# Two pieces of side work moved in a tuned decoder block: the squares of x and the batched heads' key selection

## The chip, the cores and the metric

The kernel runs on one core of one Trainium2 chip. The metric is device time of one execution, in microseconds (us). The time before is the median of three runs, and one further run was taken with the hardware profiler; every row quoted below comes from that profiled run. TensorE is PE in the profile (PEld its weight loads), VectorE is DVE, ScalarE is ACT, GpSimd is POOL, SyncE is SP.

## The reference

One decoder block over 1024 tokens of width 1024, float32. Gated linear attention (GLA) and a spatial gating branch run beside each other and are merged; behind them stands PEER, a mixer that picks 16 of 16384 one-neuron experts for each of eight heads by product keys. Cut to what matters here:

```python
h = modulate(rms_norm(x, norm1_w), shift1, scale1)      # needs mean(x*x) of every row
q, k, v, r, a_lr, su, sv, g_a, g_b = split(h @ w_in)
o = gla_chunked(q, k, v, log_sigmoid(a_lr @ w_alpha_up + b_alpha) / 16)
merged = sigmoid(g_a) * rms_norm(o) * silu(r) + sigmoid(g_b) * spatial_gating(gelu(su), gelu(sv))
x = x + gate1 * (merged @ w_out)
h2 = modulate(rms_norm(x, norm2_w), shift2, scale2)
# PEER: scores of two key halves, top 16 of each, top 16 of the sums, softmax, experts
s1, s2 = q1 @ keys1.T, q2 @ keys2.T                     # q1, q2 = halves of h2 @ w_q, 8 heads
v1, i1 = top_k(s1, 16); v2, i2 = top_k(s2, 16)
top_s, pos = top_k(v1[:, None] + v2[None, :], 16)
y = sum(softmax(top_s) * gelu(u_idx . h2) * v_idx)
out = rms_norm(x + gate2 * y, final_norm_w)
```

## The kernel before, in words

The tokens are worked in two halves of 512 (`hf` 0 and 1), each as four blocks of 128. Every projection is a **group**: 512 output columns, eight steps k over the 1024 inputs, four PSUM tiles. A step loads a 128x512 weight tile `wt` (SP queue, line 1250), splits it into `wh` (ACT, line 1253) and `wl` (DVE, line 1254), and runs twelve matmuls. The split runs three steps ahead (`LOOK`), with four buffers each for the loads and for the split tiles. Behind the eighth step come the four evictions, and the next group's matmuls need the PSUM tiles that these free.

One half runs, in this order: value groups V0 and V1; query/key groups QK0 and QK1, each followed by two GLA heads; the gating groups; the output projection; and then the four **query groups** of PEER, `w_q(0)` to `w_q(3)`. A query group's evictions copy PSUM to `qt` on ACT (line 1607); `s_part` multiplies `qt` by the keys (line 1655, PSUM pool `aux`, two buffers), copies the scores to `so` (line 1657) and selects the best eight of each key half on DVE (lines 200, 201).

`x_prep` gets the second half's first norm ready inside the first half. It loads four blocks of x as rows (`xb`, line 1175), squares each on ACT with a row sum (line 1176), turns the sums into one reciprocal root per token (`rstd_row`: DVE and POOL, a matmul into `aux` at line 1165, a copy to `rrow` at line 1167), loads x transposed (`xt`, line 1182) and multiplies it by `rrow` on DVE (line 1184, eight products). At the start of the second half `h_split` turns these into `hTh` (ACT, line 1211) and `hTl` (DVE, lines 1215 and 1216), which the value group V0 reads. Before the change the whole of `x_prep` is called behind `w_q(1)`.

The selection of experts has two ways. Most heads take at most eight of each key half (`route`); a (token, head) pair whose eighth weight still counts is gathered into a batch of 128 such pairs per half, and `rare` does a full top-16 for them: it builds the list, fetches their scores from DRAM into `qsc` by an indirect DMA on POOL (line 428), runs `tops16` on both key halves (lines 204 to 208), then `select16`, `gates` and `pack_rare`, whose result goes to DRAM (lines 293 and 294) and is read back at line 507 when `peer_stream` opens.

The order on each engine comes from three things. Generators (`route`, `pack_half`, `rare` in the queue `qr`; `direct_rows` in `qdir`; `peer_stream` in `qp`) are advanced by `step()`, behind each step k of a group, and `qr` runs its first generator only; so the program order of side work is fixed by counts of steps. The tile framework's scheduler then takes the program order as priority and places each instruction on its engine by its own timeline. And `tc.issue_after(ins)` puts the block's instructions behind `ins` in the order of that instruction's engine; it orders issue, it is no wait of its own. What comes out is one fixed order for each engine, in which each instruction waits for its inputs.

`direct_rows`, which computes each token's first expert of every head, uses the same pool of eight row buffers (`b4`) as `xb` and fetches two 512 KB tiles for each head (line 752).

Of the kernel before, what the change touches and what calls it, by code (L numbers as in the profile page):

```python
# [17 lines left out]
P = 128  # L18
# [62 lines left out]
def block_kernel(ctx: ExitStack, tc: tile.TileContext, x, xT, cT, w_ada, b_ada, b_adaT, n1T, w_inp, w_alr,  # L81
# [256 lines left out]
    def route(hf, q, tsel, tv, ti):  # L338
# [48 lines left out]
        nc.vector.tensor_copy(tsel[:, :, c0:c0 + 2 * K1], w[:, :, 0].rearrange("p (b k) -> p b k", b=BH))  # L387
        yield

    def rare(gi, rps):  # L390
        nb = len(GROUPS[gi])
        n, col = nb * PH, NBLK + NG + gi
        f = flags[gi].rearrange("p b h -> p (b h)")
        inc = r2.tile([P, n], F32, name="qinc")
        tq = r2.tile([P, n + 4], F32R, name="tq")
        nc.vector.tensor_tensor_scan(inc, ones[:, :n], f, 0.0, op0=OP.mult, op1=OP.add)
        nc.vector.tensor_tensor(tq[:, 0:n], inc, f, op=OP.mult)
        nc.vector.tensor_copy(cnt[:, col:col + 1], inc[:, n - 1:n])
        pst = rps.tile([P, 1], F32, name="aux", tag="aux")
        nc.tensor.matmul(pst, ltri, cnt[:, col:col + 1], start=True, stop=True)  # L400
        se = r2.tile([P, 2], F32, name="qse")
        nc.vector.tensor_copy(se[:, 0:1], pst)
        nc.vector.tensor_tensor(se[:, 1:2], se[:, 0:1], cnt[:, col:col + 1], op=OP.add)
        nc.scalar.activation(tq[:, n:n + 1], se[:, 0:1], AF.Identity, scale=-1.0)
        nc.scalar.activation(tq[:, n + 1:n + 2], lane1, AF.Identity, bias=-1.0)
        nc.scalar.activation(tq[:, n + 2:n + 4], ones[:, 0:2], AF.Identity)
        lt = r2.tile([P, P], F32, name="qlt", tag="cidx")
        E = r2.tile([P, P], F32R, name="qE", tag="th")
        nc.vector.tensor_scalar(lt, iota[:, :P], se[:, 1:2], None, op0=OP.is_lt)
        nc.vector.scalar_tensor_tensor(E, iota[:, :P], se[:, 0:1], lt, op0=OP.is_ge, op1=OP.mult)  # L410
        yield
        tps = rps.tile([P, n + 4], F32, name="tpq", tag="aux")
        nc.tensor.matmul(tps, E, tq, start=True, stop=True)
        tt = r2.tile([P, n + 4], F32, name="qt")
        nc.scalar.activation(tt, tps, AF.Identity)
        r = r2.tile([P, 4], F32, name="qr")
        nc.vector.tensor_tensor(r[:, 0:1], tt[:, n:n + 1], lane1, op=OP.add)
        nc.vector.scalar_tensor_tensor(inc, tt[:, 0:n], r[:, 0:1], ctab[:, :nb].rearrange("p b h -> p (b h)"),
                                       op0=OP.is_equal, op1=OP.mult, accum_out=r[:, 1:2])
        nc.vector.scalar_tensor_tensor(r[:, 2:3], tt[:, n + 1:n + 2], float(PH), r[:, 1:2], op0=OP.mult, op1=OP.add)  # L420
        ix = r2.tile([P, 1], I32, name="qix")
        nc.vector.tensor_copy(ix, r[:, 2:3])
        nc.vector.tensor_scalar(rtok[gi], ix, 3, None, op0=OP.logical_shift_right)
        nc.vector.tensor_copy(r[:, 3:4], rtok[gi])
        for i in range(nb):
            nc.vector.tensor_scalar(rcol[gi][:, i:i + 1], r[:, 3:4], -float(i * P), None, op0=OP.add)
        sc = rp.tile([P, 2, NK], F32, name="qsc", tag="bits")
        nc.gpsimd.indirect_dma_start(out=sc.rearrange("p c k -> p (c k)"), out_offset=None,
                                     in_=s_g[gi].rearrange("b p (h k) -> (b p h) k", h=PH),
                                     in_offset=bass.IndirectOffsetOnAxis(ap=ix, axis=0))  # L430
        yield
        tv = r2.tile([P, 1, 2, TOPK], F32, name="qtv")
        ti = r2.tile([P, 1, 2, TOPK], U32, name="qti")
        for c in range(2):
            tops16(tv[:, 0, c], ti[:, 0, c], sc[:, c])
        yield
        ts, sel = yield from select16(r2, tv, ti, 1, "q")
        tsel = r2.tile([P, 3 * TOPK + 2], F32, name="qtsel")
        dd, sm = yield from gates(r2, ts, 1, TOPK, "q")
        nc.vector.tensor_tensor(sm, sm, tt[:, n + 2:n + 3], op=OP.mult)  # L440
        nc.vector.tensor_scalar(tsel[:, 2 * TOPK:3 * TOPK], dd[:, 0], sm, None, op0=OP.mult)
        nc.vector.scalar_tensor_tensor(tsel[:, TOPK:2 * TOPK], sel[:, 0], float(NK), sel[:, 1], op0=OP.mult, op1=OP.add)
        yield
        yield from pack_rare(tsel, TOPK, NBLK + gi, rps, "q")
        yield
# [607 lines left out]
    with ExitStack() as pa:  # L1053
# [113 lines left out]
            nc.scalar.activation(rrow, rps, AF.Identity)  # L1167
            return rrow

        def x_prep(t0):  # L1170
            ss = sm_p.tile([P, BH], F32, name="ss")
            for i in range(BH):
                xb = t4("xb")
                with tc.issue_after(last_wt[0]):
                    nc.sync.dma_start(xb, x[t0 + i * P:t0 + (i + 1) * P, :])
                nc.scalar.activation(xb, xb, AF.Square, accum_out=ss[:, i:i + 1])
            rrow = rstd_row(ss, nc.vector)
            xts = []
            for k in range(0, KD, 2):
                xt = v4.tile([P, 2, HALF], F32, name="xt", tag="v4")  # L1180
                with tc.issue_after(last_wt[0]):
                    nc.sync.dma_start(xt, xT[k * P:(k + 2) * P, t0:t0 + HALF].rearrange("(a p) t -> p a t", p=P))
                for kk in range(2):
                    nc.vector.tensor_tensor(xt[:, kk], xt[:, kk], rrow, op=OP.mult)
                    xts.append(xt[:, kk])
            return xts
# [50 lines left out]
            at.append(a)  # L1237

        order_ = (G_V0, G_V1, G_QK0, G_QK1, G_SV0, G_SV1, G_R0, G_R1, G_A0, G_A1, G_SU0, G_SU1, G_B0, G_B1)
        plan, made, last_wt = [], [], []  # L1240
        for _ in range(NHALF):
            plan += [(w_inp[g], k) for g in order_ for k in range(KD)]
            plan += [(w_outp[m], k) for _ in range(2) for k in range(KD) for m in range(2)]
# [13 lines left out]
        for hf in range(NHALF):  # L1257
# [108 lines left out]
            def ev_qk(hp):  # L1366
                def f(i, ps):
                    h = 2 * hp + i % 2
                    G, eg, p4 = G16[h], eglt[h], v4c(ps)

                    def last(c):
                        return eg[:, :, c:c + 1].to_broadcast([P, 4, 64])

                    if i < 2:
                        eG = t2("eG")
                        with tc.issue_after(last_vt[0]):
                            nc.scalar.activation(eG, G, AF.Exp, scale=1.0 / TAU)
                        e4 = v4c(eG)
                        qs = gl.tile([P, HALF], F32, name="qs")
                        q1 = gl.tile([P, 4, 64], F32, name="q1")  # L1380
                        q4 = v4c(qs)
                        nc.vector.scalar_tensor_tensor(q4[:, :, 0], p4[:, :, 0], DK ** -0.5, e4[:, :, 0], op0=OP.mult, op1=OP.mult)
                        nc.vector.scalar_tensor_tensor(q1, p4[:, :, 1], DK ** -0.5, e4[:, :, 1], op0=OP.mult, op1=OP.mult)  # L1383
                        nc.vector.tensor_tensor(q4[:, :, 1], q1, last(0), op=OP.mult)
                        qk[h] = [qs, q1]
                    else:
                        kk = gl.tile([P, 4, 3, 64], F32, name="kk")
                        kt = gl.tile([P, HALF], F32, name="kt", bufs=1)
                        k4 = v4c(kt)
                        G3 = G.rearrange("p (c s) -> p c s", s=64)  # L1390
                        dt_ = t2("dt")
                        nc.vector.tensor_tensor(dt_.rearrange("p (c s) -> p c s", s=64),
                                                G3[:, :, 63:64].to_broadcast([P, 8, 64]), G3, op=OP.subtract)
                        eGi = t2("eGi")
                        with tc.issue_after(last_vt[0]):
                            nc.scalar.activation(eGi, G, AF.Exp, scale=-1.0 / TAU)
                            nc.scalar.activation(dt_, dt_, AF.Exp, scale=1.0 / TAU)
                        d4 = v4c(dt_)
                        nc.vector.tensor_tensor(kk[:, :, 0:3:2], p4, v4c(eGi), op=OP.mult)
                        nc.vector.tensor_tensor(kk[:, :, 1], p4[:, :, 0], d4[:, :, 0], op=OP.mult)  # L1400
                        nc.vector.tensor_tensor(k4[:, :, 1], p4[:, :, 1], d4[:, :, 1], op=OP.mult)
                        nc.vector.tensor_tensor(k4[:, :, 0], kk[:, :, 1], last(1), op=OP.mult)
                        qk[h] += [kk, kt]
                return f

# [196 lines left out]
            def w_q(q, half=None):  # L1602
                qts = [None] * 4
                if half is None:
                    def ev(m, ps):
                        qts[m] = t2("qt")
                        nc.scalar.activation(qts[m], ps, AF.Identity)

                    group(w_qp[q], ev, True)
                else:  # L1610
# [64 lines left out]
            for q in range(1, 4):  # L1675
# [1 line left out]
                    rate["p"] = RP3  # L1677
                w_q(q)
                if hf == 0 and q == 1:
                    xts = x_prep(HALF)  # L1680
            qa.drain()
    behind.append(last_s[0])
    use.append(peer_pools("1", "left", UVC, 1, 2, AH, EB, True))
# [78 lines left out]
```

## Time and profile before

| what | us |
|---|---|
| three runs | 1449.78, 1451.9, 1454.23 |
| median | 1451.9 |
| the profiled run, its own time | 1450.17 |
| the span that its trace covers | 1448.4 |
| PE busy in the span | 1348.1 |
| DVE busy | 1091.7 |
| ACT busy | 737.9 |
| POOL busy | 278.7 |

The span lies inside the run's own time; 1.8 us lie around it. The profile's page gives busy time per engine, the granted TensorE clock in slices, the chain of work that ended last, and groups of instructions by line. The trace behind it can be asked for one engine's instructions in order of time (the timeline), for who waited for whom (the waits), for the instructions of one tile, and for busy time in chosen stretches (the windows). A row of the timeline reads: start in us, duration in us, engine and line, operation, tile written and tiles read, shape, count, and in brackets the engine's idle time before it with what ended that. A busy PE in a window doesn't say at what clock it ran: the granted clock stands in a column of its own (1.00 is full speed).

### The profile page before, as it was taken

The numbers are of one execution on the slowest core, as the hardware profiler recorded it, in microseconds if no ns is written. First come the engines' busy times: TensorE is split into PE (matmuls) and PEld (weight loads), VectorE is DVE, ScalarE is ACT, GpSimd is POOL, SyncE is SP. The second block draws the span as 40 slices with busy tenths as digits, with TensorE's granted clock in tenths as the row PEclk, the third lists the DMA queues.
The fourth block names the chain that finished last, engine by engine and source line by source line (L and its number), as shares of the span: only waits on it lengthen the run. The fifth ranks groups of instructions, "written<-read, shape, count | busy, mean of one in ns | idle before, by whom it ended". The sixth has DMA issues, their size and how long they took to land.

```text
span 1448.4 us, 19642 instructions
## 1 busy us (share of the span) xinstructions
PE 1348.1 (93%) x6004; PEld 1039.6 (72%) x6004; DVE 1091.7 (75%) x3114; ACT 737.9 (51%) x1611; POOL 278.7 (19%) x275
## 2 busy tenths in 40 slices
PE   3999999999999889997989999999988999789996
PEld 2778877888888778776868787887766886445553
DVE  6584768443468669988879888778889877799775
ACT  4454333333255456474534677556645555556542
POOL 0100001000000011422442133221111024443331
PEclk8899999999999999998999999999998999999999
DMA  9552454322258484757587689796687669987984
GB/s 321 184 214 95 170 184 161 105 95 88 88 171 280 160 291 168 265 177 275 194 308 263 222 325 343 286 354 216 219 324 264 227 216 356 355 347 303 419 331 166
DMA packets 120836, 345.00 MB, mean 238 GB/s; under 512 B 15033, under 2 KB 24505, under 8 KB 108690
## 3 DMA queue, kind: packets, MB, share of 16 engines
q0 software_dynamic: 32064, 165.95, 30.7%
q1 hardware_dynamic: 70992, 133.20, 26.8%
q10 hardware_dynamic: 17666, 44.53, 8.5%
q8 instruction: 48, 0.79, 0.2%
q14 instruction: 66, 0.54, 0.1%
HBM read 319.40 MB, written 24.23 MB: 237 GB/s over the span
## 4 chain that ended last, share of the span: by engine, by line
PE 41%; DMA 8%; DVE 7%; issue 5%; ACT 4%; POOL 1%; ACTq 0%; DVEq 0%; POOLq 0%
PE acc L606 7%; PE mm L181 6%; PE mm L182 6%; PE mm L184 6%; DMA uv<-in_tab_dram,ix 4%; PE mm L187 3%; PE mm L188 3%; PE mm L189 3%; PE aux L1655 2%; PE hps L578 1%; DMA wt<-in_w_inp_dram 1%; PE hps L579 1%; DVE wl L1254 1%; DVE uv L580 1%; DMA xb<-in_x_dram 1%
## 5 line engine op out<-in xcount | busy, mean ns | idle before, releaser
L1253 ACT ACTIVATE wh<-wt 128x512 fp32r<-128x512 f32 x368 | 228.2, 628 | 322.9 <-PE mm L182 133.5
L1254 DVE TENSOR_TENSOR wl<-wt,wh 128x512 fp32r<-128x512 f32 x368 | 247.7, 685 | 137.1 <-ACT wh L1253 73.2
L181 PE MATMUL mm<-wh,hTh 128*128 128x512 f32 x672 | 265.9, 398 | 3.1 <-ACT wh L1253 3.1
L182 PE MATMUL mm<-wh,hTl 128*128 128x512 f32 x672 | 263.8, 395 | 0.0
L184 PE MATMUL mm<-wl,hTh 128*128 128x512 f32 x672 | 207.6, 394 | 0.0
L181 PEld LDWEIGHTS mm<-wh,hTh 128*128 128x128 f32 x672 | 127.1, 189 | 35.0 <-ACT wh L1253 4.8
L182 PEld LDWEIGHTS mm<-wh,hTl 128*128 128x128 f32 x672 | 126.9, 189 | 27.1 <-issue 1.0
L184 PEld LDWEIGHTS mm<-wl,hTh 128*128 128x128 f32 x672 | 125.6, 188 | 27.0 <-DVE wl L1254 0.6
L525 POOL DMA_INDIRECT uv<-in_tab_dram,ix x74 | 80.4, 1086 | 262.9 <-ACT ix L557 178.3
L187 PE MATMUL mm<-wh,hTh 128*128 128x512 f32 x224 | 90.5, 413 | 8.4 <-ACT hTh L1211 5.5
L182 PE MATMUL mm<-hTl,wh 128*128 128x512 f32 x240 | 96.5, 402 | 0.0
L181 PE MATMUL mm<-hTh,wh 128*128 128x512 f32 x240 | 95.9, 400 | 0.0
L580 DVE SCALAR_TENSOR_TENSOR uv<-uv,hps 128x512 f32<-128x512 f32 x112 | 74.8, 679 | 24.5 <-DMA uv<-in_tab_dram,ix 16.8
L188 PE MATMUL mm<-wl,hTh 128*128 128x512 f32 x224 | 89.1, 398 | 0.1
L189 PE MATMUL mm<-wh,hTl 128*128 128x512 f32 x224 | 88.4, 397 | 0.0
L187 PE MATMUL mm<-hTh,wh 128*128 128x256 f32 (+1 forms) x208 | 71.6, 346 | 10.7 <-DVE q L1383 7.6
L188 PE MATMUL mm<-hTl,wh 128*128 128x256 f32 (+1 forms) x208 | 69.8, 337 | 3.0 <-DVE hTl L173 3.0
L184 PE MATMUL mm<-hTh,wl 128*128 128x512 f32 x240 | 71.4, 398 | 0.0
L752 POOL DMA_INDIRECT uvd<-in_down_dram,dix x32 | 37.1, 1159 | 177.8 <-DVE cidx L353 40.0
L618 DVE SCALAR_TENSOR_TENSOR vl<-uv,r,vh 128x512 fp32r<-128x512 f32 x84 | 61.3, 745 | 10.6 <-ACT vh L617 7.7
L189 PE MATMUL mm<-hTh,wl 128*128 128x256 f32 (+1 forms) x208 | 68.9, 337 | 0.0
L578 PE MATMUL hps<-hh,E 128*128 128x512 f32 x132 | 62.4, 473 | 4.5 <-DVE uv L580 3.6
(938 smaller groups left out, 2875.3 us busy)
## 6 DMA issues: line engine op xcount, KB each, us to landing
wt<-in_w_inp_dram SPq DMA_DIRECT2D x224, 256.0 KB, 3.5
wt<-in_w_qp_dram SPq DMA_DIRECT2D x80, 256.0 KB, 3.0
wada<-in_w_ada_dram SPq DMA_DIRECT2D x32, 512.0 KB, 4.8
wt<-in_w_outp_dram SPq DMA_DIRECT2D x64, 256.0 KB, 3.5
wada<-in_w_ada_dram SPq DMA_DIRECT2D x32, 256.0 KB, 5.8
s_d<-so ACTq DMA_DIRECT2D x28, 256.0 KB, 5.3
xr<-in_x_dram ACTq DMA_DIRECT2D x8, 512.0 KB, 6.5
x_d<-x ACTq DMA_DIRECT2D x8, 512.0 KB, 4.4
```

What stands on the lines that cost most here:

```text
L181: nc.tensor.matmul(ps, lh, rh, start=False, stop=False)
L182: nc.tensor.matmul(ps, *((lh, rl) if feat else (ll, rh)), start=False, stop=False)
L184: nc.tensor.matmul(ps, *((ll, rh) if feat else (lh, rl)), start=False, stop=False)
L187: nc.tensor.matmul(ps, lh, rh, start=first, stop=False)
L188: nc.tensor.matmul(ps, lh, rl, start=False, stop=False)
L189: return nc.tensor.matmul(ps, ll, rh, start=False, stop=last).ins
L525: nc.gpsimd.indirect_dma_start(out=dst[:], out_offset=None, in_=src, in_offset=off)
L578: nc.tensor.matmul(hps, Ej, hh[:, sl], start=True, stop=False)
L580: nc.vector.scalar_tensor_tensor(uv[0][:, sl], uv[0][:, sl], 1.0, hps, op0=OP.mult, op1=OP.mult, accum_out=r[:, 2 + n:3 + n])
L606: ins = nc.tensor.matmul(acc[:, sl], W, v[:, sl], start=first, stop=last).ins
L1253: nc.scalar.activation(wh, wt, AF.Identity)
L1254: nc.vector.tensor_tensor(wl, wt, wh.bitcast(F32), op=OP.subtract)
```

## The change

Two edits.

The first splits `x_prep`. A new `x_load` issues the four loads of `xb` behind `w_q(1)`, as before. The squares and all that follows, the loads of `xt` among it, are called behind `w_q(2)`, and the squares are put behind the last `qt` eviction so far (`last_qt`) in ACT's order.

The second holds `rare` back. Behind the gather of `qsc` it yields until `crit` holds an instruction: the last operation of the second half's QK0 evictions for head 1 (line 1402). For the first half's batch (`gi` 0) `tops16` is also put behind that instruction in DVE's order. The second half's batch finds `crit` filled and runs as before.

```diff
+    crit = []
+
     def rare(gi, rps):
...
         yield
+        while not crit:
+            yield
         tv = r2.tile([P, 1, 2, TOPK], F32, name="qtv")
         ti = r2.tile([P, 1, 2, TOPK], U32, name="qti")
-        for c in range(2):
-            tops16(tv[:, 0, c], ti[:, 0, c], sc[:, c])
+        with nullcontext() if gi else tc.issue_after(crit[0]):
+            for c in range(2):
+                tops16(tv[:, 0, c], ti[:, 0, c], sc[:, c])
         yield
...
-        def x_prep(t0):
-            ss = sm_p.tile([P, BH], F32, name="ss")
+        def x_load(t0):
+            xbs = []
             for i in range(BH):
                 xb = t4("xb")
                 with tc.issue_after(last_wt[0]):
                     nc.sync.dma_start(xb, x[t0 + i * P:t0 + (i + 1) * P, :])
-                nc.scalar.activation(xb, xb, AF.Square, accum_out=ss[:, i:i + 1])
+                xbs.append(xb)
+            return xbs
+
+        def x_prep(t0, xbs):
+            ss = sm_p.tile([P, BH], F32, name="ss")
+            for i, xb in enumerate(xbs):
+                with tc.issue_after(last_qt[0]):
+                    nc.scalar.activation(xb, xb, AF.Square, accum_out=ss[:, i:i + 1])
             rrow = rstd_row(ss, nc.vector)
...
-                        nc.vector.tensor_tensor(k4[:, :, 0], kk[:, :, 1], last(1), op=OP.mult)
+                        kl = nc.vector.tensor_tensor(k4[:, :, 0], kk[:, :, 1], last(1), op=OP.mult)
+                        if hf and not crit and h % 2:
+                            crit.append(kl.ins)
...
-                        nc.scalar.activation(qts[m], ps, AF.Identity)
+                        last_qt[:] = [nc.scalar.activation(qts[m], ps, AF.Identity).ins]
...
                 if hf == 0 and q == 1:
-                    xts = x_prep(HALF)
+                    xbs = x_load(HALF)
+                if hf == 0 and q == 2:
+                    xts = x_prep(HALF, xbs)
```

More of the change, by code (lines that the diff above doesn't have):

```diff
@@ L1239, in block_kernel @@
         order_ = (G_V0, G_V1, G_QK0, G_QK1, G_SV0, G_SV1, G_R0, G_R1, G_A0, G_A1, G_SU0, G_SU1, G_B0, G_B1)
-        plan, made, last_wt = [], [], []
+        plan, made, last_wt, last_qt = [], [], [], []
         for _ in range(NHALF):
```

## The prediction

> **What bounds the kernel now.** First the page: the busy shares (part 1), then the waits, those of PE alone.
>
> ```profile
> PE 1348.1 (93%) x6004; PEld 1039.6 (72%) x6004; DVE 1091.7 (75%) x3114; ACT 737.9 (51%) x1611; POOL 278.7 (19%) x275
> PE mm L187 <- DVE q L1383: 7.6, 1, 7.6
> PE aux L1655 <- ACT qt L1607: 4.2, 1, 4.2
> ```
>
> PE is busy 93% of the span, so time is won where PE waits or runs slowly. Among PE's nine longest waits two are single events that lie where the two edits are: 7.6 us until a DVE eviction of QK0, 4.2 us until an ACT eviction of a query group. Then the chain of waits in order of time, and the timelines of PE and ACT around the second event.
>
> ```profile
> 508.96 11.75 DMA xb<-in_x_dram
> 522.94 1.22 PE aux L1655 x4
> 524.16 0.43 PE mm L187
> 527.58 0.27 PE mm L184
> 527.85 0.45 PE aux L1655 x4
> 528.29 0.23 PE mm L187
> ...
> 518.30 0.39 PE L189 MATMUL mm<-hTh,wl 128*128 128x512 f32 x1
> 522.94 1.22 PE L1655 MATMUL aux<-keyst,qt 128*128 128x128 f32 x4 [4.25 <-ACT qt L1607]
> 520.74 1.06 ACT L1176 ACTIVATE xb<-xb 128x1024 f32<-128x1024 f32 x1 [1.42 <-DMA xb<-in_x_dram]
> 522.31 2.04 ACT L1607 ACTIVATE qt<-mm 128x512 f32<-128x512 f32 x4
> 520.00:525.00 5.00, 2.06 (x7) 1.87 (x8) 2.61 (x5) 4.24 (x8) 1.05 (x1) 0.57 1.04 392
> ```
>
> `w_q(1)` starts its last matmul at 518.30, yet its four evictions run at 522.31: ahead of them on ACT stand the four squares (the last is quoted), each waiting for its own `xb`, which crosses the DMA engines at 1.04 of their time. PE restarts at 522.94 and is slow at first: in the last row (windows: length; busy of PE, PEld, DVE, ACT, POOL; granted clock; DMA share; GB/s) the clock is 0.57, and the chain's matmul pieces are 0.43 us, then 0.23 from 528.29.
>
> **The first edit, what it removes.** Between the starts at 518.30 and 522.94 lie 4.64 us where 0.23 would do: 4.4 lost. From 522.94 to 527.85 one set of score matmuls and nine matmul pieces take 4.91 us; at the later pace 0.45 + 9 x 0.23 = 2.52: 2.4 lost. If the squares go, the evictions follow the matmuls and PE runs on: **6.8 us**. That this handover can be free shows in the next one, where no square stands in the way:
>
> ```profile
> 552.04 0.58 ACT L1607 ACTIVATE qt<-mm 128x512 f32<-128x512 f32 x1
> 556.46 1.08 ACT L1657 ACTIVATE so<-aux 128x512 f32<-128x512 f32 x2 [0.66 <-PE aux L1655]
> 550.00:560.00 10.00, 10.00 (x54) 8.54 (x53) 9.73 (x43) 9.05 (x16) 0.00 (x0) 1.00 0.69 248
> 500.00:530.00 30.00, 4.60 (x8) 0.89 0.83 305
> ```
>
> PE is busy 10.00 of 10 at full clock there. (The last row is a window of the tile `xb` alone: 4.60 us of ACT for the four squares and their sums.) I go on in the old run's times; the whole moves about 6.8 earlier.
>
> **What it adds.** The squares now stand behind 552.62, the end of that last `qt`; their rows landed some 30 us before, so they wait for nothing. Their 4.6 us run from 552.6 to 557.2. In order behind them on ACT are the copies `so` (556.46 before, so 0.8 late) and the splits `wh`; `aux` comes free later, and `w_q(3)`'s matmuls cover that. ACT's 9.05 of 10 loses two `hTh` that can't come so early now (below), so it isn't over-full. I cost it at 0; without the cover it is the 0.8.
>
> The work behind the squares is what the move can hurt:
>
> ```profile
> 544.17 0.86 PE aux L1165 x2
> 545.70 5.03 DVE L1184 TENSOR_TENSOR xt<-xt,rrow 128x512 f32<-128x512 f32 x8 [0.24 <-ACT rrow L1167]
> 537.53 0.60 ACT L1657 ACTIVATE so<-aux 128x512 f32<-128x512 f32 x1 [0.50 <-PE aux L1655]
> 558.67 1.51 ACT L1211 ACTIVATE hTh<-xt,mod,scol 128x512 fp32r<-128x512 f32 x2
> 564.20 0.58 ACT L1657 ACTIVATE so<-aux 128x512 f32<-128x512 f32 x1
> 565.75 1.29 DVE L1216 TENSOR_TENSOR hTl<-xt,hTh 128x512 fp32r<-128x512 f32 x2
> 576.88 0.40 PE L187 MATMUL gaux<-hTh,walr_h 128*16 128x512 f32 x1
> 522.17 1.05 POOL L169 TENSOR_TENSOR rstd<-rstd,mhalf 128x4 f32<-128x4 f32 x1 [9.41 <-DVE rstd L168]
> ```
>
> The matmul of line 1165 needs an `aux` buffer behind `w_q(2)`'s four scores, so it can't come before their last copy, 564.20 + 0.58 + the 0.8 = 565.6 (POOL's 1.05 of work is done by then; no gather stands in its queue). Before, it came at 544.17, 6.0 behind the copy of `w_q(1)` that ended at 538.1; the same again gives 571.6. Behind it, by these rows: 0.9 matmul, 0.6 `rrow`, 5.0 for all eight products in one run as now, 0.6 for the first `hTl` (its `hTh`, 0.8, falls beside the products): 7.1, so 572.7 to 578.7. PE first reads it at 576.88, so it costs between 0 and 1.8 at its near end, with a far end that is rival B; I take **+0.9**, the middle. DVE gets no more work, but 5.0 us of it move from 545 into a stretch that is full.
>
> The queues passed: SP still gets `xb` at once, but the four `xt` loads (2 MB) go one group later, in front of `w_q(3)`'s weights instead of `w_q(2)`'s.
>
> ```profile
> 514.30 3.46 SPq L1250 DMA_DIRECT2D wt<-in_w_qp_dram  x1
> DMA to landing us min/median/max: 2.6/3.0/14.0
> 530.00:540.00 10.00, 10.00 (x54) 8.57 (x53) 9.68 (x40) 4.89 (x10) 0.00 (x0) 1.00 0.45 160
> ```
>
> The weight behind them now is issued at 514.30; if it is the 14.0 of the tile's landing times, it lands at 528.3, and PE, busy 10.00 of 10 from 530 to 540, doesn't wait for it. One group later only four gathers come along instead of `xb` and four gathers, so the same lead holds: 0. [...]
>
> **The second edit.** The timelines of DVE, ACT and PE, and the work on `qsc` in a window:
>
> ```profile
> 657.10 0.49 DVE L204 MAX8 qtv<-qsc 128x8 f32<-128x128 f32 x2 [3.19 <-DMA qsc<-s_d,qix]
> 657.67 0.69 DVE L1254 TENSOR_TENSOR wl<-wt,wh 128x512 fp32r<-128x512 f32 x1
> 657.01 0.63 ACT L1253 ACTIVATE wh<-wt 128x512 fp32r<-128x512 f32 x1 [4.86 <-DMA wt<-in_w_inp_dram]
> 664.77 0.42 DVE L1382 SCALAR_TENSOR_TENSOR qs<-mm,eG 128x256 f32<-128x256 f32 x1
> 665.66 0.77 PE L187 MATMUL mm<-hTh,wh 128*128 128x512 f32 x1 [7.58 <-DVE q L1383]
> 657.60:664.77 7.17, 1.06 (x6) 0.00 (x0) 0.71 1.04 407
> 690.00:700.00 10.00, 9.27 (x47) 7.42 (x45) 6.32 (x22) 7.03 (x16) 1.81 (x2) 1.00 0.72 240
> ```
>
> DVE stands 3.19 us for the gather of `qsc`, and PE then 7.58 for DVE. But the 3.19 are shadowed: the next instruction, `wl`, needs the `wh` that ends at 657.64 because its weight was late, and it starts at 657.67. Taking `tops16` away leaves DVE waiting there to the same moment. What goes is the batch's work between 657.6 and the eviction at 664.77: 1.06 us, no more, since the rest of those 7.2 us are `yd`, `uvd` and `wl` that stay. **1.1 us**; bounds 0 and the whole 7.6 plus its slow stretch. The slow stretch stays, for 6.5 us of waiting are left.
>
> What is moved comes back behind line 1402 while the GLA heads run, PE idle 0.73 in ten there. The batch's pieces are small, but each can delay a head. Bounds are 0 and the 7.6 that it stood in before; I take 0.7, that stretch's PE idle, the row nearest to it. Its result is needed late:
>
> ```profile
> 693.85 0.33 ACTq L293 DMA_DIRECT2D ts_d<-thq  x1
> 756.90 0.33 ACTq L507 DMA_DIRECT2D thl<-ts_d  x1
> ```
>
> 63 us lie between; `rare` has eight steps in QK1 and two in the next group, so I expect it to be written near 740, still in time: 0.
>
> **The sum:** -6.8 + 0 + 0.9 + 0 - 1.1 + 0.7 = **-6.3 us**. Span 1448.4 to 1442.1; with the 1.8 around it the profiled run's 1450.17 becomes 1443.9. The median of the runs shown is 1.7 above the profiled run, so I forecast 1451.9 - 6.3 = **1445.6**.
>
> **The rivals.**
>
> A: *the handover is freed only by half.* A square or a late weight still stands ahead of an eviction, or the later `hTl` hold PE a little. 2.2 of the stall stay. A row bears on the slow stretch:
>
> ```profile
> 472.76 3.66 PE L1655 MATMUL aux<-keyst,qt 128*128 128x128 f32 x16 [2.12 <-ACT qt L1623]
> ```
>
> There 2.1 us of waiting are followed by 16 records in 3.66 us, where the chain's 0.45 for four makes 1.8: slow after a short wait too. So 2.4 stay as well, and the gain is 2.2 less 0.5 (0.9 - 1.1 + 0.7): 1450.2. [...]
>
> B: *slower: x comes late to V0.* The place is the matmul of line 1165 in PE's order. If the scheduler sets it behind all of `w_q(3)`, at 576.9, then the 7.1 us pass before the first `hTl`, and 0.8 for an `hTh` that can't run beside the products if they are split up, and PE's next instruction (576.88) reads it, the scores being queued behind. So long a stall brings the slow stretch, 2.4, and the next three steps' `hTl`, 0.6 each behind DVE's full queue, some 2: 12.3. In place of the 0.9 that is 5.1 slower, 1457.0. It decides from a matmul later than 576.88 - 7.1 = 569.8. For it: it came 22 us behind the squares before, where 566 to 572 is 8 to 14. Against: it waited for `aux` then too.
>
> C: *QK0's evictions come up at once.* If the scheduler, free of `tops16`, sets them ahead of `yd` and `uvd`, they start at 658.3, not 664.8; 6.5 less 1.1 more, and 2.4 of slow stretch: 1437.8. Against: those operations come earlier in the program and keep their priority.
>
> The change doing nothing is no rival: the squares leave ACT's order ahead of the evictions by construction; only the order around them is open.
>
> **How the numbers follow.** Forecast 0.50, A 0.25, B 0.14, C 0.11. About 0.3%, 4.4 us, can be told from no change: faster is below 1447.5, slower above 1456.3. Faster takes C, 0.43 of the forecast's 0.50 and 0.04 of A: 0.58. Slower is most of B: 0.13. The rest, 0.29, is within. The range leaves out most of B and a little beyond C: 1437.0 to 1454.0.
>
> **What would show it.** Right: no wait of PE on `qt` L1607 beside `w_q(1)`, clock 1.00 in the windows there, squares without a DMA wait; PE busy through the start of V0; the QK0 wait near 6.5. Wrong: a PE wait on `hTh` or `hTl` at V0 (B), a QK0 wait below 2 (C), `thl` read later against the QK groups than 63 us minus the delay allowed.

## The result, and the profile after

| | before | after |
|---|---|---|
| median, us | 1451.12 (14 runs, 1444.44 to 1460.37) | 1458.62 (14 runs, 1451.36 to 1465.05) |
| the profiled run, us | 1450.17 | 1464.19 |
| its span, us | 1448.4 | 1462.4 |

The ratio of after to before is 1.0058 (95%: 1.0039 to 1.0076): slower by 8.4 us (5.7 to 11.0, the ratio times 1451). The forecast was 6.3 us faster, its range ended at 1454.0. The two profiled runs lie 14 us apart: that of after is 5.6 us above its kernel's median, that of before 0.9 below. Places can be compared in them, the sum can't.

The new kernel's lines stand 12 to 14 lower: `wh` is line 1265, `qt` 1621, the scores 1669, `hTl` 1228, the gathers of `direct_rows` 757. The page and PE's waits after:

```profile
PE 1352.7 (93%) x6004; PEld 1040.7 (71%) x6004; DVE 1092.9 (75%) x3114; ACT 733.4 (50%) x1609; POOL 289.7 (20%) x275
PE aux L1669 <- ACT qt L1621: 8.1, 4, 3.9
PE mm L187 <- ACT wh L1265: 7.3, 4, 5.9
PE mm L189 <- DVE hTl L1228: 3.7, 1, 3.7
```

The single wait on `qt` of 4.2 us is down to 1.6 at its place, but the same pair of lines now waits 8.1 us in four places, the wait at QK0 is 5.9 instead of 7.6 and ends on a late `wh`, and a wait on `hTl` is new. Where the time comes from is read off the start of each group's first eviction on ACT. The two runs start at different paces, so each is counted from the last eviction of `w_q(0)` (495.56 before, 492.98 after):

| first eviction of | before | after | after is |
|---|---|---|---|
| `w_q(1)` | 26.8 | 21.1 | 5.6 earlier |
| `w_q(2)` | 54.1 | 48.4 | 5.7 earlier |
| `w_q(3)` | 79.7 | 83.1 | 3.5 later |
| V0, second half | 107.2 | 114.9 | 7.7 later |
| V1, second half | 139.8 | 148.3 | 8.5 later |

So the handover that the edit aimed at gave 5.6; the stretch from there to `w_q(3)`'s first eviction lost 9.2, and that to V0's 4.3. Two profiled runs of one kernel (the second edit alone, below) differ by up to 2.1 us in this count. Behind V1 the difference doesn't stand still: counted the same way at the splits `wh` on ACT, after is between 0.3 us ahead of before and 14.9 behind. So the 8.5 us at V1 lie close to the 8.4 of the ratio, but the traces don't carry them to the end. First the handover from `w_q(1)`: the timelines of ACT and PE and a window.

```profile
514.11 1.96 ACT L1621 ACTIVATE qt<-mm 128x512 f32<-128x512 f32 x3 [0.91 <-PE mm L189]
519.57 0.63 ACT L1265 ACTIVATE wh<-wt 128x512 fp32r<-128x512 f32 x1 [3.50 <-DMA wt<-in_w_qp_dram]
521.62 0.58 ACT L1621 ACTIVATE qt<-mm 128x512 f32<-128x512 f32 x1
522.25 0.71 PE L1669 MATMUL aux<-keyst,qt 128*128 128x128 f32 x4 [1.59 <-ACT qt L1621]
520.00:525.00 5.00, 3.41 (x18) 2.61 (x18) 3.60 (x8) 4.51 (x9) 0.00 (x0) 1.00 0.52 191
```

Three evictions now follow the matmuls. The fourth stands behind a split `wh` whose weight is late among the `xb` loads and the gathers; PE waits 1.59 us for it, and the clock stays at 1.00. Then the handover from `w_q(2)`: the queues of SP and POOL, ACT, PE and two windows.

```profile
531.76 2.93 SPq L1194 DMA_DIRECT2D xt<-in_xT_dram  x4
535.67 2.36 SPq L1262 DMA_DIRECT2D wt<-in_w_qp_dram  x2
535.30 0.94 POOL L757 DMA_INDIRECT uvd<-in_down_dram,dix  x1 [25.12 <-DVE dix L1654]
539.03 0.94 POOL L757 DMA_INDIRECT uvd<-in_up_dram,dix  x1 [0.30 <-issue]
541.36 1.96 ACT L1621 ACTIVATE qt<-mm 128x512 f32<-128x512 f32 x3 [0.95 <-PE mm L189]
549.09 0.63 ACT L1265 ACTIVATE wh<-wt 128x512 fp32r<-128x512 f32 x1 [5.77 <-DMA wt<-in_w_qp_dram]
549.74 1.28 ACT L771 ACT_TABLE_LOAD   x1
551.14 0.58 ACT L1621 ACTIVATE qt<-mm 128x512 f32<-128x512 f32 x1
551.77 0.71 PE L1669 MATMUL aux<-keyst,qt 128*128 128x128 f32 x4 [3.86 <-ACT qt L1621]
545.00:550.00 5.00, 2.91 (x17) 2.21 (x15) 0.25 (x1) 0.89 (x2) 0.00 (x0) 1.00 0.77 297
550.00:555.00 5.00, 3.23 (x12) 2.63 (x13) 3.03 (x5) 4.99 (x10) 0.00 (x0) 0.77 0.16 55
```

The four `xt` loads and, within some 8 us, the group's four gathers stand in front of the weights that are issued from 535.67 on. One of those weights is so late that its split waits 5.77 us on ACT, ahead of a table load and of the fourth `qt`. PE waits 3.86 for that, is busy 6.14 of these 10 us, where it was busy throughout before, and the clock goes to 0.77.

Not all of the 9.2 us are this stall. PE begins the last step of `w_q(3)` at 572.53, 79.6 us behind `w_q(0)`, where before it was at 574.16 and 78.6; so 6.7 us are lost up to there. The other 2.5 stand on ACT, as the timelines of PE and ACT show:

```profile
572.53 0.39 PE L187 MATMUL mm<-hTh,wh 128*128 128x512 f32 x1
571.36 2.92 ACT L1223 ACTIVATE hTh<-xt,mod,scol 128x512 fp32r<-128x512 f32 x4
574.71 1.50 ACT L1223 ACTIVATE hTh<-xt,mod,scol 128x512 fp32r<-128x512 f32 x2
576.12 1.53 ACT L1621 ACTIVATE qt<-mm 128x512 f32<-128x512 f32 x3
576.75 0.71 PE L1669 MATMUL aux<-keyst,qt 128*128 128x128 f32 x4 [1.10 <-ACT qt L1621]
```

The `hTh` of the second half, which need the products, now run in front of `w_q(3)`'s evictions. The first eviction comes 3.6 us behind the start of that last step, against 1.1 before, and PE waits 1.10 us for it. Last, V0: the timelines of DVE, POOL and PE.

```profile
569.42 4.88 DVE L1196 TENSOR_TENSOR xt<-xt,rrow 128x512 f32<-128x512 f32 x8
569.86 5.25 POOL L757 DMA_INDIRECT uvd<-in_up_dram,dix  x1 [0.30 <-DMA wt<-in_w_inp_dram]
575.41 1.87 POOL L757 DMA_INDIRECT uvd<-in_down_dram,dix  x1 [0.30 <-issue]
582.71 1.23 DVE L769 SCALAR_TENSOR_TENSOR uvd<-uvd,h2d 128x1024 f32<-128x1024 f32 x1 [2.67 <-DMA uvd<-in_down_dram,dix]
585.66 2.49 DVE L1228 TENSOR_TENSOR hTl<-xt,hTh 128x512 fp32r<-128x512 f32 x4
586.40 1.72 PE L189 MATMUL mm<-wh,hTl 128*128 128x512 f32 x4 [3.69 <-DVE hTl L1228]
```

The products of `xt` end at 574.3, as early as the forecast had them. But the first `hTl` runs at 585.66, because on DVE a dot of `direct_rows` (line 769) stands ahead of it and waits 2.67 us for its gather, which was issued at 575.41 behind a gather whose issue lasted 5.25 us where others last 0.94. From the start of `w_q(3)`'s last step to V0's first eviction, where the late x chain acts on ACT and on DVE, the changed kernel takes 35.4 us, before 28.6: 6.8 are lost.

### The profile page after: what moved, and what is told of

Same layout as the page of the kernel before. It is cut to its first block, busy times and chain, and to the rows that moved or that the text cites. A ratio compares the mean times of both kernels' runs of the same rounds, so it can differ in the third digit from the quotient of the medians.

```text
span 1462.4 us, 19662 instructions
## 1 busy us (share of the span) xinstructions
PE 1352.7 (93%) x6004; PEld 1040.7 (71%) x6004; DVE 1092.9 (75%) x3114; ACT 733.4 (50%) x1609; POOL 289.7 (20%) x275
## 4 chain that ended last, share of the span: by engine, by line
PE 32%; DVE 11%; DMA 5%; issue 5%; ACT 3%; POOL 0%; ACTq 0%; DVEq 0%; POOLq 0%
PE acc L611 5%; PE mm L181 5%; PE mm L182 5%; PE mm L184 5%; PE mm L187 2%; PE mm L188 2%; PE mm L189 2%; DVE uv L585 1%; DMA uv<-in_tab_dram,ix 1%; DMA fin<-y_d 1%; PE hps L583 1%; DVE wl L1266 1%; PE hps L584 1%; DVE uv L539 1%; PE aux L1669 1%
## 5 line engine op out<-in xcount | busy, mean ns | idle before, releaser
L530 POOL DMA_INDIRECT uv<-in_tab_dram,ix x74 | 84.4, 1140 | 268.3 <-ACT ix L562 162.5
L585 DVE SCALAR_TENSOR_TENSOR uv<-uv,hps 128x512 f32<-128x512 f32 x112 | 75.0, 683 | 15.5 <-DMA uv<-in_tab_dram,ix 6.9
L622 ACT ACTIVATE vh<-uv,r 128x512 fp32r<-128x512 f32 x84 | 57.8, 716 | 21.8 <-PE acc L630 8.6
```

The costliest lines, as they stand in the source:

```text
L530: nc.gpsimd.indirect_dma_start(out=dst[:], out_offset=None, in_=src, in_offset=off)
L585: nc.vector.scalar_tensor_tensor(uv[0][:, sl], uv[0][:, sl], 1.0, hps, op0=OP.mult, op1=OP.mult, accum_out=r[:, 2 + n:3 + n])
```

## The experiments

T1 was the theory ahead of the first four: the `xt` loads in front of `w_q(3)`'s weights, and the late x chain at V0, cost more than the freed handover gives, and the second edit does about nothing. T2: the second edit costs it. T3: only the scheduler's new order does. All ratios are to the kernel before on the same chip, and every time in us behind a ratio is its excess over 1 times 1452.

| kernel | median, us | before, us | ratio (95%) |
|---|---|---|---|
| first edit alone | 1469.39 | 1455.29 | 1.0107 (1.0065 to 1.0149) |
| second edit alone | 1451.15 | 1455.29 | 0.9977 (0.9954 to 1.0001) |
| second edit alone, again | 1446.24 | 1452.81 | 0.9967 (0.9940 to 0.9993) |
| after, `xt` loads at the old place | 1454.57 | 1455.29 | 1.0006 (0.9979 to 1.0033) |
| before, only `xt` loads and products later | 1462.56 | 1452.81 | 1.0070 (1.0036 to 1.0105) |
| before, squares behind `w_q(1)`'s last eviction | 1463.26 | 1455.29 | 1.0042 (1.0013 to 1.0071) |
| the same, products set apart | 1451.10 | 1452.81 | 1.0000 (0.9978 to 1.0021) |
| the same, and the second edit | 1454.40 | 1452.81 | 1.0020 (0.9997 to 1.0043) |
| before, `xb` loads a group earlier | 1454.00 | 1450.95 | 1.0025 (1.0000 to 1.0050) |
| the same, and the second edit | 1467.08 | 1450.95 | 1.0106 (1.0057 to 1.0155) |
| before, an Identity ahead of each square | 1461.21 | 1450.95 | 1.0072 (1.0043 to 1.0100) |

**Each edit alone.** The first kernel is the changed one without the `crit` lines:

```diff
-        while not crit:
-            yield
...
-        with nullcontext() if gi else tc.issue_after(crit[0]):
-            for c in range(2):
-                tops16(tv[:, 0, c], ti[:, 0, c], sc[:, c])
+        for c in range(2):
+            tops16(tv[:, 0, c], ti[:, 0, c], sc[:, c])
```

> Only the first edit, the second undone. T1 (the xT loads, moved in front of the fourth query group's weights, and the late x chain at V0 cost more than the freed handover gains; the second edit does about nothing): 5 to 10 us slower than before, ratio 1.0035 to 1.007, PE again waiting about 3.9 us on a qt eviction at the end of w_q(2) and about 3.7 us on hTl at V0. T2 (the second edit costs the 7.5, by its batched pieces among the GLA heads): 2 to 6 us faster than before, ratio 0.996 to 0.9985. T3 (neither place matters, the scheduler's new order happens to be worse somewhere later): no place of the trace with a loss by the start of V0 of more than 2 us.

The second is the kernel before with just these lines in their changed form, and was run twice.

> Only the second edit on the kernel before. T1: within 3 us of before, ratio 0.998 to 1.002, with the trace the same up to the start of V0. T2: 5 to 10 us slower, ratio 1.0035 to 1.007, lost between QK0's evictions and the gates.

> The second edit alone a second time, since its first interval (0.9954 to 1.0001) just holds no change. If its gain is real: 2 to 5 us faster, and the two together exclude 1. If not: within 1.5 us of before. The price of 0.4 forecast for it would be too small in the first case, by the wait of PE on QK0's eviction, 5.55 us where before had 7.58.

Measured: the first edit alone 15.5 us slower (9.4 to 21.6), beyond T1's range too; the second 3.3 and 4.8 us faster. T2 falls: the second edit is worth more than the 0.4 forecast, and the first costs more than the whole. In the trace of the first edit alone the waits don't stand as T1 put them, 3.9 us at the handover from `w_q(2)` and 3.7 on `hTl`. PE's timeline has 3.03 at the handover from `w_q(1)` and 1.32 at that from `w_q(2)`:

```profile
523.60 1.22 PE L1666 MATMUL aux<-keyst,qt 128*128 128x128 f32 x4 [3.03 <-ACT qt L1618]
552.15 0.71 PE L1666 MATMUL aux<-keyst,qt 128*128 128x128 f32 x4 [1.32 <-ACT qt L1618]
```

At that from `w_q(3)` it is 2.71, and 1.90 on `hTl` at V0. V0's first eviction is 6.4 us later than before, which T3 excluded; V1's is 7.2 later, so about half of the 15.5 comes behind it, at places not found. At QK0 the second edit alone shows, on PE, DVE and ACT:

```profile
661.74 0.76 PE L187 MATMUL mm<-hTh,wh 128*128 128x512 f32 x1 [5.55 <-DVE q L1388]
654.71 0.69 DVE L1259 TENSOR_TENSOR wl<-wt,wh 128x512 fp32r<-128x512 f32 x1 [2.92 <-ACT wh L1258]
654.05 0.63 ACT L1258 ACTIVATE wh<-wt 128x512 fp32r<-128x512 f32 x1 [4.02 <-DMA wt<-in_w_inp_dram]
```

The wait is 5.55 instead of 7.58. In the second profiled run of the same kernel it is 6.64, and there a late weight's split ends it:

```profile
665.45 0.77 PE L187 MATMUL mm<-hTh,wh 128*128 128x512 f32 x1 [6.64 <-ACT wh L1258]
```

The kernel with the first edit alone, which leaves `tops16` in its place, has 5.36. So these waits don't show how much the second edit gains at QK0. The shadow was there: without `tops16`, DVE stands 2.92 us at the same place for the split of a late weight.

**The `xt` loads back.** The changed kernel, but the loads of `xt` go out with those of `xb`, behind `w_q(1)`:

```diff
         def x_load(t0):
...
+            for k in range(0, KD, 2):
+                xt = v4.tile([P, 2, HALF], F32, name="xt", tag="v4")
+                with tc.issue_after(last_wt[0]):
+                    nc.sync.dma_start(xt, xT[k * P:(k + 2) * P, t0:t0 + HALF].rearrange("(a p) t -> p a t", p=P))
+                xt2.append(xt)
+            return xbs, xt2
```

> The changed kernel with both edits, but the four xT loads issued with the xb loads behind the second query group as in the kernel before; squares, row factor and products stay behind the third. T1: wh no longer waits for a late weight ahead of the third group's last eviction; about 9 us come back there, the 4 at V0 stay or shrink: 1 us slower to 6 faster than before, ratio 0.996 to 1.001. T2: still 5 to 10 us slower. A variant of T1 in which the gathers and not the xT loads make the weight late: the wait stays, still 5 or more slower.

Measured: 0.9 us over before; against the changed kernel's 1.0058 that is 7.6 us less (2.8 to 12.3, by the two intervals). The place agrees: PE's wait at the handover from `w_q(2)` is 0.54, and PE begins the last step of `w_q(3)` 72.8 us behind `w_q(0)`, 6.8 ahead of the changed kernel and 5.8 ahead of before. T1's total held, and the variant in which the gathers alone make the weight late is out. But of the 9 us that T1 wanted back at that place only 4.6 are there at `w_q(3)`'s first eviction (78.5 us behind `w_q(0)`, where the changed kernel had 83.1), because the `hTh` on ACT hold it up for longer:

```profile
574.04 0.71 PE L1673 MATMUL aux<-keyst,qt 128*128 128x128 f32 x4 [3.23 <-ACT qt L1625]
```

From the start of that last step to V0's first eviction this kernel takes 9.1 us more than before. So in its trace the late x chain takes all that the freed handover had given, and V0 is 3.2 us later than before.

**The `xt` loads alone.** The kernel before; squares and handover as they were, but loads and products one group later:

```diff
-                    xts = x_prep(HALF)
+                    xrr = x_prep(HALF)
+                if hf == 0 and q == 2:
+                    xts = x_mul(HALF, xrr)
```

> The kernel before with one part of the first edit: the xT loads and the products that need them one group later, in front of the fourth query group's weights; squares and the handover as before. T1 (these 2 MB make a weight late at the handover from the third to the fourth group): a wh or qt wait of 3 us or more there, 4 to 10 us slower than before, ratio 1.003 to 1.007. Rival (the loads only hurt because the freed handover has brought the weights and gathers closer to them): within 2 us of before.

Measured: 10.2 us slower (5.2 to 15.2), just over T1's range, and not at the place that T1 gave. Its PE, a window, DVE and PE again:

```profile
523.36 1.22 PE L1657 MATMUL aux<-keyst,qt 128*128 128x128 f32 x4 [6.40 <-ACT qt L1609]
550.00:555.00 5.00, 5.00 (x26) 4.21 (x25) 4.72 (x12) 2.01 (x4) 0.00 (x0) 1.00 1.03 402
613.87 1.23 DVE L764 SCALAR_TENSOR_TENSOR uvd<-uvd,h2d 128x1024 f32<-128x1024 f32 x1 [2.53 <-DMA uvd<-in_down_dram,dix]
618.52 0.79 PE L188 MATMUL gaux<-all__5473,wal_h 16*128 16x512 f32 x1 [3.00 <-DVE all__5473 L173]
```

At the handover from `w_q(2)` PE is busy 5.00 of 5: no late weight holds it there. So the stall in the changed kernel takes both, the moved loads and gathers that come earlier (535.30 there, 543.92 here); with the loads back the gathers come early too, and it isn't there either. Behind V0 PE waits for `all_`, which stands on DVE behind a dot that waits for its gather. The 6.40 at the first handover are no sign of the loads: the two runs of the second edit alone have 4.92 and 6.23 there. V1's first eviction is 6.9 us later than before; what makes the 10.2 is not shown.

**The handover alone.** The kernel before, with the squares behind `w_q(1)`'s own last eviction and nothing else moved. The cut is against the changed kernel; its second edit is left out as well:

```diff
-                    xbs = x_load(HALF)
-                if hf == 0 and q == 2:
-                    xts = x_prep(HALF, xbs)
+                    xts = x_prep(HALF, x_load(HALF))
```

> The kernel before with one thing changed: the squares stand behind the second query group's last eviction (same group as before, all loads, products and the row factor where they were). T1: the handover w_q(1) to w_q(2) is freed as in the changed kernel (5 to 8 us by its trace) and nothing is paid for it: 3 to 7 us faster than before, ratio 0.995 to 0.998. T3: no gain, within 2 us. If the handover's gain is mostly eaten by the rest of the overfull stretch behind it (DVE, gathers), 0 to 2 us faster.

Measured: 6.1 us slower, and no stated outcome was right. The handover is free (first eviction of `w_q(2)` 6.7 us ahead of before), and at `w_q(3)` all of it is gone (0.5 behind). The timelines of DVE, POOL, ACT and PE and a window show how:

```profile
542.93 4.89 DVE L1193 TENSOR_TENSOR xt<-xt,rrow 128x512 f32<-128x512 f32 x8
543.77 4.86 POOL L754 DMA_INDIRECT uvd<-in_up_dram,dix  x1 [0.30 <-issue]
548.94 2.95 POOL L754 DMA_INDIRECT uvd<-in_down_dram,dix  x1 [0.30 <-DVE ts L359]
556.01 1.23 DVE L766 SCALAR_TENSOR_TENSOR uvd<-uvd,h2d 128x1024 f32<-128x1024 f32 x1 [4.62 <-DMA uvd<-in_down_dram,dix]
557.28 0.20 ACT L768 ACTIVATE rdr<-rdr 128x1 f32<-128x1 f32 x1 [5.96 <-DVE uvd L766]
559.59 3.78 PE L1666 MATMUL aux<-keyst,qt 128*128 128x128 f32 x16 [3.38 <-ACT so L1668]
560.00:565.00 5.00, 5.00 (x21) 4.61 (x21) 5.00 (x27) 3.71 (x8) 0.00 (x0) 0.50 0.47 164
```

Read down: a gather is issued while DVE runs its eight products, and its issue lasts 4.86 us; the next is issued at 548.94; the dot that needs it stands 4.62 us; ACT's `rdr` behind the dot stands 5.96, ahead of the copies `so`; PE waits 3.38 for them and then runs at a clock of 0.50. In the kernel before the products run there too, and gathers are issued beside them, each in 0.94:

```profile
546.30 0.94 POOL L752 DMA_INDIRECT uvd<-in_up_dram,dix  x1 [0.30 <-ACT wh L1253]
547.55 0.94 POOL L752 DMA_INDIRECT uvd<-in_down_dram,dix  x1 [0.30 <-issue]
```

**The products set apart.** As the last kernel, with each pair of products behind a weight split in the first four steps of `w_q(3)`:

```diff
-                for kk in range(2):
-                    nc.vector.tensor_tensor(xt[:, kk], xt[:, kk], rrow, op=OP.mult)
...
+                def mul(xt=xt):
+                    with tc.issue_after(last_wl[0]):
+                        for kk in range(2):
+                            nc.vector.tensor_tensor(xt[:, kk], xt[:, kk], rrow, op=OP.mult)
+
+                post[(0, 1, 2, 3)[k // 2]] = mul
```

> As the kernel with the squares behind the second query group's last eviction, which came out 0.42% slower with the handover freed; here its eight products of xt are set in pairs behind the weight splits of the fourth group's first steps, instead of in one run while the four gathers are issued. G (the gather whose issue lasted 4.86 us beside that run made the next gathers, a dot on VectorE, an so copy on ScalarE and the scores on PE late, and so took the gain back): every gather issue of that stretch near 1 us again, no wait of PE on so there, 2 to 7 us faster than before, ratio 0.995 to 0.9985. O (the stretch behind the handover is full in any case, and the time won is lost to VectorE and the gathers whatever the products' place): slower by 3 to 9 us again, ratio 1.002 to 1.006.

Measured: the time of before, 6.1 us (0.9 to 11.3) less than with the products in one run. All four issues are short, as POOL's timeline shows for two:

```profile
546.62 0.94 POOL L754 DMA_INDIRECT uvd<-in_up_dram,dix  x1 [0.30 <-issue]
547.86 0.94 POOL L754 DMA_INDIRECT uvd<-in_down_dram,dix  x1 [0.30 <-DVE pos L360]
```

The gathers don't run beside the products here: their issues end at 550.0, and the products run from 553.6 to 570.0. G held for the place: no wait on `so`, and V1's first eviction comes 133.4 us behind `w_q(0)`, 6.4 ahead of before. It failed for the end: nothing of these 6.4 is left there. In its profiled run, the slowest of its twelve, the lead is still 9.6 us at the 265th of the 368 splits `wh`, in the gating groups, and gone at the 301st, in the output projection.

> The same with the second edit beside it. If both gains hold and add: 5 to 10 us faster than before, ratio 0.993 to 0.9965. If the second edit's gain is only that of its own scheduler order: the same as without it, within 2 us.

Measured: 0.2% slower than before (0.03% faster to 0.43% slower). The first outcome is out: the second edit's gain doesn't show here. From the kernel without the second edit it is 2.9 us off, 4.6 either way, which can't be told from nothing.

**The rows earlier.** The kernel before, with only the four `xb` loads issued one group earlier:

```diff
+            if hf == 0:
+                xbs = x_load(HALF)
             for q in range(1, 4):
```

> The kernel before with only the four xb loads issued one group earlier, behind the first query group; squares, xT loads and products where they were. H (the squares held the handover because their rows were late, not because they are in the way): squares without a DMA wait, wait of PE on qt there below 2 us, w_q(2)'s evictions some 5 earlier against the first group's last eviction. To the end: 2 to 6 us faster if an early gain is kept; within 3 us of before if such a gain is lost behind it, as where the products were set apart. Rival: the 2 MB only move the late weight one group forward, 0 to 5 us slower.

Measured: 3.6 us slower (0 to 7.3), inside the rival's range and outside H's. H held for the handover (PE's wait 1.54, first eviction of `w_q(1)` 4.5 us earlier; only the first square still waits for its row, 1.53). But a gather issued beside the products lasts 5.76 us, and DVE's waits on gathers between 500 and 720, by the waits view of each kernel's own trace, grow from the first row (before) to the second:

```profile
DVE uvd L764 <- DMA uvd<-in_down_dram,dix: 4.0, 4, 1.7
```

```profile
DVE uvd L766 <- DMA uvd<-in_down_dram,dix: 14.2, 6, 3.9
```

> The same with the second edit. If the second edit's 4 us add to whatever the earlier rows give: 4 us faster than that kernel, 4 to 10 faster than before. If the second edit pays only in the kernel before's own order (it did nothing beside the products set apart): within 2 us of that kernel.

Measured: 15.4 us slower than before, 11.8 more than without the second edit. Neither outcome was right. V1's first eviction is 0.2 us later than before, so this loss lies behind it.

**The squares twice.**

```diff
+                nc.scalar.activation(xb, xb, AF.Identity)
                 nc.scalar.activation(xb, xb, AF.Square, accum_out=ss[:, i:i + 1])
```

> The kernel before with an Identity over xb ahead of each square, four more ScalarE operations of some 1.05 us in front of w_q(1)'s evictions, that is a known delay of 1 to 4 us at the handover (the operations fit partly into the waits for the rows). K (what is lost in this stretch is kept to the end): 1 to 5 us slower than before, ratio 1.001 to 1.0035. S (a shift here is taken up by slack further on, so gains at the handover are worth little too): within 1 us of before.

Measured: 10.5 us slower, twice K's upper end, though the first eviction of `w_q(1)` is only 0.6 us later, and that of V1 3.6. What that small shift did stands on DVE and POOL:

```profile
544.51 4.90 DVE L1185 TENSOR_TENSOR xt<-xt,rrow 128x512 f32<-128x512 f32 x8
544.68 5.61 POOL L752 DMA_INDIRECT uvd<-in_down_dram,dix  x1 [19.73 <-DVE ts L359]
```

The first gather of the group, issued 0.17 us behind the start of the products instead of 0.71 ahead of it, lasts 5.61, and the three behind it are late; `w_q(3)` begins to evict 5.3 us later.

## Why the prediction was wrong, by its steps

**The handover, -6.8.** Right in mechanism, a little large: 5.6. The slow stretch went with the stall, as forecast; a late weight in front of the fourth eviction kept 1.59 us of waiting. Rival A had taken the slow stretch to stay, from the row with 2.12 us of waiting; here 1.59 us are followed by a clock of 1.00, while 3.38 and 3.86 are followed by 0.50 and 0.77. Two rows lie between: behind the rival's 2.12 the clock is 0.55 (before, window from 472.7 to 476.5), and in the kernel with the `xt` loads back, where PE waits 2.23 us at V0, it is 0.67 in the window from 585 to 590. What sets the clock behind a wait these five rows don't show.

**The squares behind `w_q(2)`, 0.** Right: they wait for nothing; none of the four, which start from 551.6 to 554.7 in the trace of after, has idle time of ACT in front of it.

**The `xt` loads, "the same lead holds: 0".** This step failed: 6.7 us at its place in the changed kernel, 7.6 (2.8 to 12.3) at the end by taking it back. Making it alone cost 10.2, but not at this place. It compared how much data comes along, "only four gathers", and not when. The gathers follow `dix`, so with the freed handover they came 7.1 us earlier, counted from `w_q(0)` (544.99 before, 535.30 after), while the `xt` loads went 23.9 later (510.41 and 531.76): the two met in front of the same weights. And it asked whether PE waits for the weight, not what stands behind its split in ACT's order, the fourth `qt`. In the trace of after the first weight behind the 2 MB is issued at 535.67, and the split that waits 5.77 us starts at 549.09, 13.4 later. The step had named the place, "in front of `w_q(3)`'s weights", and still priced it at 0.

**The x chain, +0.9.** This step failed too, by about as much: 6.8 us at its place in the changed kernel, 9.1 with the `xt` loads back, 6.6 with the first edit alone. No run changes it alone, so this is read from traces. The matmul and the products came in time, the matmul at 565.73 where rival B decides from 569.8. What failed is the path behind the products. The forecast let the `hTh` fall beside them and saw two `hTh` leave ACT, but not that they would stand there in front of `w_q(3)`'s evictions, where PE then waits 1.10 us, 2.71 and 3.23 in the three kernels. And `hTl` was costed by its own 0.6 us, but stands on DVE behind a dot that waits for a gather; PE waits 3.69 for it. A wait on `hTl` at V0 was the sign named for rival B, which had the place and the sign, by another mechanism.

**What no step had.** The forecast moved the eight products on DVE and asked only what DVE has to do there, not what POOL issues beside them. In all profiled runs of this study, thirteen of them:

| kernels | the eight products on DVE, us | longest issue of the group's four gathers, us |
|---|---|---|
| before; second edit alone, twice | in one run, 5.03; 5.01, 5.03 | 1.01 |
| after; first edit alone; `xt` loads back | in one run, 4.88 each | 5.25 each |
| handover alone; rows earlier, without and with the second edit; squares twice | in one run, 4.89; 4.90, 4.91; 4.90 | 4.86; 5.76, 5.76; 5.61 |
| products apart, without and with the second edit | in ones and twos, behind the gathers | 1.01, 1.01 |
| `xt` loads alone | in ones and twos, beside the gathers | 1.04 |

Each long issue ends 0.8 to 1.8 us behind the run of products. No gather's issue of over 4 us stands anywhere else in the thirteen traces. Setting the products apart made the issues short and gave 6.1 us back (0.9 to 11.3), 8.1 at V1. That fits the collision as the cost, but the edit also puts the products 7 to 19 us later, counted from `w_q(0)`, and elsewhere the end moved by as much with V1 in its place, so the size isn't shown by itself; nor is the cause. In the three runs in which the gathers pass beside one run of products (before; the second edit alone, twice), these take 0.10 to 0.15 us longer (5.01 to 5.03 against 4.88 to 4.91), and the gathers come through within the run.

**The second edit, -0.4.** Right in sign and in the shadow, too small: 3.3 and 4.8, with intervals from -0.1 to 6.7 and 1.0 to 8.7. The wait at QK0 that it forecast near 6.5 is 5.55 in one of its runs and 6.64 in the other, so the gain isn't shown to arise there. In the changed kernel `thq` is written at 728.25 and read at 762.80, in time as forecast.

**What stays open.** Where the second edit's gain arises, and why it is lost beside the products apart (0.2% slower instead of 0.3% faster) and turns over beside the earlier rows. And why the 6.4 us that the products apart have won by V1 don't reach the end. A place by V1 doesn't settle the end in these kernels: the second edit alone, faster at the end, is 0.5 and 2.6 us later there, and the one that ends 15.4 slower 0.2. The order on every engine far behind the change differs from kernel to kernel, and the profiled runs of one kernel differ too. T3 may hold for that part; it wasn't tested by itself. The kernel before with the second edit alone is the only version whose median ratio is clearly below 1, in the second of its two measurements.

## What to carry to other kernels

When a stall is removed, follow each thing that its end had been timing, here the gathers' issue, and look at what it meets at its new time; a load that is moved the other way may meet it in front of the same weights. On engines with a fixed order, price a late transfer by what stands behind the instruction that waits for it, not by who reads it. And before moving elementwise work on VectorE, look at what GpSimd issues in that stretch: in seven of the ten traces with an uninterrupted run a gather's issue beside it took about as long as the run itself (4.86 to 5.76 us beside 4.88 to 4.91), and with the squares twice the first gather went from 0.71 us ahead of the products to 0.17 behind them and was held up. Last, price a producer's work not only by when it is read: moved late, it stands in front of other things on its own engine, here the `hTh` in front of the evictions.

## What the hardware showed that wasn't expected

In seven of the ten traces in which DVE runs the eight 128x512 products back to back, a gather's issue on POOL that comes in meanwhile lasted 4.86 to 5.76 us, against 0.94. Where the gather before it had been issued 0.7 us ahead of the first product, as in the kernel before, the next ones came through, each in 0.94; 0.47 ahead (handover alone) was not enough, and neither was 0.88 (after), so the lead alone doesn't decide.
